# Four query projections in a row: reordering the calls of the mixer stage in a hybrid decoder layer

## The chip, the cores and the metric

The kernel runs on one core of a Trainium2 chip. The metric is the device time of one execution in microseconds (us), as the median of three runs. One further execution was profiled; its time and its trace are shown below.

## What is computed

One decoder layer over 512 tokens and a model width of 1024, in float32:

```
h = x + 0.5 * swiglu(rmsnorm(x), W1)
n = rmsnorm(h);  z = n @ w_in
aq, ak, av, gq, gk, gv, glr, gog = split(z)
A: aq, ak = rope(rmsnorm per head); window attention (128) with sinks, blocks of 128 queries
B: gated linear attention, 4 heads: log_alpha from glr, chunked recurrence over q, k, v;
   rmsnorm(out) * silu(gog)
h = h + concat(A, B) @ w_out
h = h + 0.5 * swiglu(rmsnorm(h), W2)
out = h + sigmoid(rmsnorm(h) @ W_g) * rmsnorm(p @ W_p)
```

The change lies in the mixer: the attention A and the recurrence B, between the two feed-forward networks.

## The kernel before

Every weight is split into a high and a low part (`Weights.split`: a cast on ScalarE, L130, a subtraction on VectorE, L131), and every large product is three matmuls (`mm3`, L187). The split tiles live in a ring of five buffers per part (`ringp`, tags whi and wlo); raw weights are loaded by SP into two buffers. A projection of 128 tokens onto 512 columns (`gemm_ts`, L295) is 24 matmuls and reads four ring tiles.

The mixer handles the 512 tokens in four blocks of 128, called 0 to 3.

- `queries(n)` (L611): projects the queries of block n (aq, 24 matmuls), copies them to SBUF and squares them on ScalarE (L617, L540), sums the squares per head on VectorE (L542, L543), takes the power -0.5 on GpSimd (L262, tile rs_q), scales (qn, L624) and rotates them on VectorE (L551 to L554), transposes them on TensorE (qtr, L629) and copies the result (qT, L631).
- `scores(n)` (L636): scores sc on TensorE in two halves, mask added on VectorE (e, L651), row maximum (mx, L653), exponentials on ScalarE (L660), reciprocal of the sum (rd, L664), scaling of e on ScalarE (L666).
- `weighted(n)` (L669): transposes e (pt, L677), copies it (pb, L679), multiplies with the values (pv) and copies into araw (L686).
- `gla_qk(j)`: the recurrence's queries and keys. `gla_decay()` (L787): the decays qb and kd, and three pairs of transposes of kd (kdt, L801).
- `gla_level(i)` (L733), seven levels of the chunk (64, 32, ... 1): X on VectorE (L739, L740), its exponential on ScalarE (L741), two products on VectorE (L742, L743), a product gr on TensorE, and a masked copy into Ac on VectorE (fill, L767; for level 64 a copy on ScalarE). `gla_diagonal()` does the same for the diagonal (gd).
- `gla_v(t)` (L705) and `gla_gate(t)` (L712): the value projection gv and the gate projection gog of block t, 24 matmuls each. `gla_state`, `gla_out`, `gla_silu` and `gla_mix` finish the recurrence, and wo projects back.

Two things set the order. First, the program is handed to a list scheduler when it is built (`schedule_with_timeline_sim=True`, L1004): an instruction that is ready goes into its engine's queue, and among several that are ready the one that stands earlier in the program goes first. Each engine then runs its queue in that order. Second, tiles of one tag share a fixed number of buffers, and an instruction that writes a new tile needs a free one:

- psA, two PSUM banks: kvr, gqk, aq of blocks 0 and 1, gv, gog.
- psG, two PSUM banks: cum, aq of blocks 2 and 3 (L614), qtr, kdt, pv, dS, otr.
- psD, two pairs of banks: sc, gr, pt, gd, o.
- w4, four SBUF buffers: la and lb, then At (two, until the end of the recurrence), kd, X.
- sm, sixteen small tiles: sums, scales, maxima, denominators.
- e, two buffers; pb, two; qT, four, later used by the gates.

The order of the calls is written out at L860 to L900, and the change touches that list alone.

Of the kernel before, what the change touches and what calls it, by code (L numbers as in the profile page):

```python
# [140 lines left out]
def hymba_kernel(tc, A, out):  # L141
# [12 lines left out]
    def psA(name):  # L154
        return psp.tile([P, 512], F32, name=name, tag="psA", bufs=2)
# [14 lines left out]
    def psD(name):  # L170
        return halls["D"][1].tile([P, 2, 512], F32, name=name, tag="psD", bufs=2)
# [3 lines left out]
    def psG(name):  # L175
        return psp.tile([P, 512], F32, name=name, tag="psG", bufs=2)

    def w4(name):
        return w4p.tile([P, 1024], F32, name=name, tag="w4")

    def small(name, n):
        return smp.tile([P, 16], F32, name=name, tag="sm", bufs=16)[:, :n]

    def mm(o, l, r, start, stop_, **kw):
        nc.tensor.matmul(o, lhsT=l, rhs=r, start=start, stop=stop_, **kw)  # L185
# [106 lines left out]
    def tokens(t):  # L292
        return slice(t * P, (t + 1) * P)

    def gemm_ts(ps, xT, t, tiles):  # L295

        n = len(tiles)
        for j, (wh, wl) in enumerate(tiles):
            for i in range(2):
                k = 2 * j + i  # L300
                mm3(ps, (xT[0][:, k, tokens(t)], xT[1][:, k, tokens(t)]), (wh[:, i, :], wl[:, i, :]),
                    k == 0, k == 2 * n - 1)
# [228 lines left out]
    def t2(name):  # L531
        return mp.tile([P, 512], F32, name=name, tag="t2", bufs=6)

    def heads(x):
        return x.rearrange("p (a d) -> p a d", d=64)

    def head_scale(src, name):

        sq = t2(f"sq_{name}")
        nc.scalar.activation(sq, src, AF.Square)  # L540
        ss = small(f"qs_{name}", 8)
        nc.vector.reduce_sum(ss, heads(sq), AX.X)  # L542
        nc.vector.tensor_scalar_add(ss, ss, 64.0 * EPS)  # L543
        return rms_scale(ss, 8, f"q_{name}")

    def rotate(x, tab, wide, name):

        t1 = t2(f"r1_{name}")
        tt = t2(f"r2_{name}")
        cs, sn = tab  # L550
        nc.vector.tensor_mul(wide(t1, 0, 64), wide(x, 0, 64), cs(0, 64))  # L551
        nc.vector.tensor_mul(wide(tt, 0, 32), wide(x, 32, 32), sn(0, 32))
        nc.vector.tensor_mul(wide(tt, 32, 32), wide(x, 0, 32), sn(32, 32))
        nc.vector.tensor_add(t1, t1, tt)  # L554
        return t1
# [55 lines left out]
    def queries(n):  # L611
        if not aq_tiles:
            aq_tiles.extend(W.get(("aq", 0, k)) for k in (0, 2, 4, 6))
        ps = (psA, psG)[n // 2](f"aq{n}")  # L614
        gemm_ts(ps, nTm, n, aq_tiles)
        aq = t2(f"aq_{n}")
        nc.scalar.copy(aq, ps)  # L617
        rs = head_scale(aq, f"q{n}")
        qn = t2(f"qn{n}")
        qv = qn.rearrange("p (h g d) -> p g h d", h=4, g=2)  # L620
        src = aq.rearrange("p (g h d) -> p g h d", h=4, g=2)
        rb = rs.unsqueeze(2).broadcast_to([P, 8, 64])
        for g in range(2):
            nc.vector.tensor_mul(qv[:, g], src[:, g], rb[:, 4 * g:4 * g + 4, :])  # L624
        qr = rotate(qn, [lambda a, m, x=x: x[:, n, a:a + m].unsqueeze(1).broadcast_to([P, 8, m]) for x in rtab[0]],
                    lambda x, a, m: heads(x)[:, :, a:a + m], f"q{n}")
        ps = psG(f"qtr{n}")
        for k in range(4):
            nc.tensor.transpose(ps[:, tokens(k)], qr[:, tokens(k)], idn)  # L629
        qT = mp.tile([P, 512], F32, name=f"qT{n}", tag="qT", bufs=4)  # L630
        nc.scalar.copy(qT, ps)  # L631
        qTs[n] = qT.rearrange("p (a c) -> p a c", a=4)
# [3 lines left out]
    def scores(n):  # L636

        k0 = (n - 1) * P if n else 0
        nk = 256 if n else 128
        e = mp.tile([P, 8, 256], F32, name=f"e{n}", tag="e", bufs=2)  # L640
        eg = e.rearrange("p (g a) c -> p g a c", g=2)
        mxt = small(f"mx{n}", 8)
        den = small(f"den{n}", 8)
        for a in range(2):
            sc = psD(f"sc{n}_{a}").rearrange("p g (a c) -> p g a c", a=2)
            for b in range(2):
                for g in range(2):
                    gs = slice(g * 64, g * 64 + 64)
                    mm(sc[:, g, b, :nk], qTs[n][gs, 2 * a + b, :], kT[gs, k0:k0 + nk], True, True)
            half = eg[:, :, 2 * a:2 * a + 2, :nk]  # L650
            nc.vector.tensor_add(half, sc[:, :, :, :nk],  # L651
                                 amask[:, 256 - nk:].unsqueeze(1).unsqueeze(1).broadcast_to([P, 2, 2, nk]))
            nc.vector.reduce_max(mxt.rearrange("p (g a) -> p g a", g=2)[:, :, 2 * a:2 * a + 2], half, AX.X)  # L653
        negm = small(f"nm{n}", 8)
        nc.vector.scalar_tensor_tensor(negm, mxt, -1.0, nsink, ALU.mult, ALU.min)
        es = small(f"es{n}", 8)
        nc.vector.tensor_add(es, negm, sink)
        nc.scalar.activation(es, es, AF.Exp)
        for a in range(8):
            nc.scalar.activation(e[:, a, :nk], e[:, a, :nk], AF.Exp, bias=negm[:, a:a + 1],  # L660
                                 accum_out=den[:, a:a + 1])
        nc.vector.tensor_add(den, den, es)
        rden = small(f"rd{n}", 8)
        nc.vector.reciprocal(rden, den)  # L664
        for a in range(8):
            nc.scalar.activation(e[:, a, :nk], e[:, a, :nk], AF.Copy, scale=rden[:, a:a + 1])  # L666
        es_[n] = e

    def weighted(n):  # L669

        e = es_.pop(n)
        kbs = (0, 1) if n else (0,)
        pbs = []
        for kb in kbs:
            pt = psD(f"pt{n}_{kb}")
            for a in range(8):
                nc.tensor.transpose(pt[:, a // 4, tokens(a % 4)], e[:, a, kb * P:(kb + 1) * P], idn)  # L677
            pb = mp.tile([P, 2, 512], F32, name=f"pb{n}_{kb}", tag="pb", bufs=2)
            nc.scalar.copy(pb, pt)  # L679
            pbs.append(pb)  # L680
        pv = psG(f"pv{n}")
        for kb in kbs:
            for g in range(2):
                mm(pv[g * 64:g * 64 + 64, :], vr[:, n - len(kbs) + 1 + kb, g * 64:g * 64 + 64], pbs[kb][:, g],
                   kb == 0, kb == kbs[-1])
        nc.scalar.copy(araw[:, :, tokens(n)], pv.rearrange("p (a c) -> p a c", a=4))  # L686
# [18 lines left out]
    def gla_v(t):  # L705
        if not gv_tiles:
            gv_tiles.extend(W.get(("gv", 1280, k)) for k in (0, 2, 4, 6))
        ps = psA(f"gv_{t}")
        gemm_ts(ps, nTm, t, gv_tiles)
        nc.scalar.copy(gv[t], ps)  # L710
# [22 lines left out]
    def gla_level(li):  # L733
        s = LEVELS[li]
        X = w4(f"X{s}")
        Xv, bv, kv, qv = (x.rearrange("p (n c) -> p n c", c=2 * s) for x in (X, bF, kF, qF))
        ref = bv[:, :, s - 1:s].broadcast_to([P, 512 // s, s])
        lo, hi = slice(0, s), slice(s, 2 * s)
        nc.vector.tensor_sub(Xv[:, :, lo], ref, bv[:, :, lo])  # L739
        nc.vector.tensor_sub(Xv[:, :, hi], bv[:, :, hi], ref)  # L740
        last_exp[0] = nc.scalar.activation(X, X, AF.Exp)  # L741
        nc.vector.tensor_mul(Xv[:, :, lo], Xv[:, :, lo], kv[:, :, lo])  # L742
        nc.vector.tensor_mul(Xv[:, :, hi], Xv[:, :, hi], qv[:, :, hi])  # L743
        both = psD(f"gr{s}")
        psv = [both[:, p].rearrange("p (n c) -> p n c", c=64) for p in range(2)]
        for n in range(8):
            if s == 64:
                for p in range(2):
                    pr = slice(p * 64, p * 64 + 64)
                    mm(psv[p][0:64, n, :], X[pr, n * P:n * P + 64], X[pr, n * P + 64:n * P + P], True, True)  # L750
            else:
                quarters(n, psv, X, X)
        if s == 64:
            for p in range(2):
                nc.scalar.copy(At[p][0:64, :, 64:128], psv[p][0:64])
        else:
            fill(li - 1, both)
# [102 lines left out]
    gla_clear()  # L860
    for j in range(4):
        gla_qk(j)
    queries(0)
    gla_decay()
    queries(1)
    scores(0)
    gla_level(0)
    queries(2)
    scores(1)
    gla_level(1)  # L870
    weighted(0)
    queries(3)
    gla_level(2)
    scores(2)
    weighted(1)
    gla_v(0)
    gla_level(3)
    scores(3)
    weighted(2)
    gla_v(1)  # L880
    gla_level(4)
    weighted(3)
    gla_v(2)
    gla_level(5)
    gla_v(3)
    gla_level(6)
# [138 lines left out]
```

## Time and profile before

| | us |
|---|---|
| median of three runs | 1019.29 (1017.42 to 1019.44) |
| profiled execution, its own time | 1019.78 |
| its span, first to last instruction | 1018.0 |
| TensorE busy | 976.7 (96%) |
| VectorE busy | 640.6 (63%) |
| ScalarE busy | 402.1 (40%) |
| GpSimd busy | 46.5 (5%) |

Times in the rows are counted from the start of the span. The mixer runs from about 395 to 565 us. A busy time of TensorE counts pipelined matmuls and includes time at a low clock, so it is no measure of peak; where TensorE is not busy at all, it waits.

### The profile page before, as it was taken

The numbers are of one execution on the slowest core, as the hardware profiler recorded it, in microseconds if no ns is written. First come the engines' busy times: TensorE is split into PE (matmuls) and PEld (weight loads), VectorE is DVE, ScalarE is ACT, GpSimd is POOL, SyncE is SP. The second block draws the span as 40 slices with busy tenths as digits, with TensorE's granted clock in tenths as the row PEclk, the third lists the DMA queues.
The fourth block names the chain that finished last, engine by engine and source line by source line (L and its number), as shares of the span: only waits on it lengthen the run. The fifth ranks groups of instructions, "written<-read, shape, count | busy, mean of one in ns | idle before, by whom it ended". The sixth has DMA issues, their size and how long they took to land.

```text
span 1018.0 us, 12357 instructions
## 1 busy us (share of the span) xinstructions
PE 976.7 (96%) x5090; PEld 809.3 (79%) x5090; DVE 640.6 (63%) x807; ACT 402.1 (40%) x588; POOL 46.5 (5%) x58
## 2 busy tenths in 40 slices
PE   6999999999999989967999999999999999999898
PEld 5888888888888868855778879888888888888687
DVE  6485757667576675476655554667566675767653
ACT  6354333333323333564773443343323333233341
POOL 2400000000000000110001100000000000000110
PEclk9899999999999998987999999999999999999999
DMA  7843315133150142300231435243250422402231
GB/s 247 287 171 124 124 41 166 42 124 124 47 172 11 54 135 77 131 1 1 83 84 46 142 96 214 84 147 101 80 168 1 165 83 83 145 1 104 83 114 52
DMA packets 73083, 105.78 MB, mean 104 GB/s; under 512 B 5681, under 2 KB 55106, under 8 KB 73026
## 3 DMA queue, kind: packets, MB, share of 16 engines
q1 hardware_dynamic: 70722, 96.60, 28.6%
q0 software_dynamic: 2304, 8.39, 2.2%
q8 instruction: 40, 0.66, 0.3%
q14 instruction: 17, 0.14, 0.0%
HBM read 98.69 MB, written 6.29 MB: 103 GB/s over the span
## 4 chain that ended last, share of the span: by engine, by line
PE 89%; DVE 6%; DMA 2%; POOL 1%; issue 1%; ACT 1%; SPq 0%; POOLq 0%
PE pu L185 24%; PE pg L185 23%; PE pd L185 20%; PE pgt L185 4%; PE wo L185 4%; PE gog L185 2%; PE gqk L185 2%; PE gv L185 2%; PE aq L185 2%; PE kvr L185 1%; DMA h<-in_x_dram 1%; DMA wraw<-in_ffn_w_gate_dram 1%; PE pv L185 1%; PE o L185 1%; DVE h L322 1%
## 5 line engine op out<-in xcount | busy, mean ns | idle before, releaser
L130 ACT CAST whi<-wraw 128x1024 fp32r<-128x1024 f32 (+1 forms) x130 | 134.4, 1040 | 217.1 <-PE pd L185 151.4
L131 DVE TENSOR_TENSOR wlo<-wraw,whi 128x1024 fp32r<-128x1024 f32 (+1 forms) x126 | 151.7, 1208 | 71.2 <-ACT whi L130 70.1
L185 PE MATMUL pg<-nhi_f,whi 128*128 128x512 f32 (+1 forms) x384 | 142.8, 374 | 2.1 <-ACT nhi_f L255 2.1
L185 PE MATMUL pg<-nlo_f,whi 128*128 128x512 f32 (+1 forms) x384 | 143.6, 374 | 0.0
L185 PE MATMUL pu<-nlo_f,whi 128*128 128x512 f32 (+1 forms) x384 | 143.3, 373 | 0.0
L185 PE MATMUL pu<-nhi_f,wlo 128*128 128x512 f32 (+1 forms) x384 | 143.3, 373 | 0.0
L185 PE MATMUL pu<-nhi_f,whi 128*128 128x512 f32 (+1 forms) x384 | 143.1, 373 | 0.0
L185 PE MATMUL pg<-nhi_f,wlo 128*128 128x512 f32 (+1 forms) x384 | 143.0, 373 | 0.0
L185 PE MATMUL pd<-whi,ahi 128*128 128x512 f32 x312 | 122.4, 392 | 4.4 <-DVE nlo_mix L256 2.2
L185 PE MATMUL pd<-wlo,ahi 128*128 128x512 f32 x312 | 121.9, 391 | 0.0
L185 PE MATMUL pd<-whi,alo 128*128 128x512 f32 x312 | 119.9, 391 | 0.0
L322 DVE SCALAR_TENSOR_TENSOR h<-pd,h 128x512 f32<-128x512 f32 x116 | 76.8, 687 | 36.9 <-PE pd L185 36.9
L185 PEld LDWEIGHTS pg<-nhi_f,whi 128*128 128x128 f32 x384 | 72.8, 190 | 15.0 <-ACT nhi_f L255 2.5
L185 PEld LDWEIGHTS pg<-nlo_f,whi 128*128 128x128 f32 x384 | 73.0, 190 | 12.6 <-DVE nlo_f L256 0.2
L185 PEld LDWEIGHTS pu<-nhi_f,wlo 128*128 128x128 f32 x384 | 73.1, 190 | 12.5
L185 PEld LDWEIGHTS pu<-nlo_f,whi 128*128 128x128 f32 x384 | 73.0, 190 | 12.5
L185 PEld LDWEIGHTS pg<-nhi_f,wlo 128*128 128x128 f32 x384 | 72.9, 190 | 12.5
L185 PEld LDWEIGHTS pu<-nhi_f,whi 128*128 128x128 f32 x384 | 73.0, 190 | 12.4
L362 DVE TENSOR_TENSOR cb<-pu,sg 128x512 f32<-128x512 f32 x44 | 30.4, 690 | 74.3 <-PE pu L185 73.7
L130 ACT CAST whi<-draw 128x1024 fp32r<-128x1024 f32 x35 | 36.7, 1053 | 100.4 <-PE pu L185 54.7
L130 ACT CAST whi<-wpr 128x1024 fp32r<-128x1024 f32 x35 | 36.9, 1053 | 98.6 <-PE pu L185 59.0
L185 PEld LDWEIGHTS pd<-whi,ahi 128*128 128x128 f32 x312 | 58.8, 188 | 17.9 <-DVE nlo_mix L256 2.4
(242 smaller groups left out, 1466.9 us busy)
## 6 DMA issues: line engine op xcount, KB each, us to landing
wraw<-in_ffn_w_gate_dram SPq DMA_DIRECT2D x22, 1024.0 KB, 5.3
wraw<-in_ffn_w_up_dram SPq DMA_DIRECT2D x22, 1024.0 KB, 5.2
wpr<-in_ffn_w_down_dram SPq DMA_DIRECT2D x10, 1024.0 KB, 5.6
draw<-in_ffn_w_down_dram SPq DMA_DIRECT2D x10, 1024.0 KB, 5.2
wraw<-in_w_in_dram SPq DMA_DIRECT2D x8, 1024.0 KB, 5.0
wraw<-in_ple_w_gate_dram SPq DMA_DIRECT2D x4, 1024.0 KB, 4.9
h<-in_x_dram SPq DMA_DIRECT2D x4, 512.0 KB, 8.5
emb_d<-eo POOLq DMA_DIRECT2D x4, 512.0 KB, 10.8
```

Of the source, the lines that this page charges most:

```text
L130: nc.scalar.copy(hi, v)
L131: (nc.gpsimd if u in (2, 3) else nc.vector).tensor_tensor(lo, v, hi.bitcast(F32), op=ALU.subtract)
L185: nc.tensor.matmul(o, lhsT=l, rhs=r, start=start, stop=stop_, **kw)
L322: nc.vector.scalar_tensor_tensor(hs, x, 0.5, hs, ALU.mult, ALU.add)
L362: nc.vector.tensor_mul(cb[:, half].rearrange("p a c -> p (a c)"), pu, sg)
```

## The change

The four calls of `queries` stand together directly behind the four calls of `gla_qk`, ahead of `gla_decay`. The calls of `gla_v` follow earlier ones by one step: `gla_v(0)` stands ahead of level 2 instead of ahead of level 3, `gla_v(1)` ahead of `scores(3)`, `gla_v(2)` ahead of `weighted(3)`. The gates stay last. No function changes.

```diff
     for j in range(4):
         gla_qk(j)
-    queries(0)
+    for n in range(4):
+        queries(n)
     gla_decay()
-    queries(1)
     scores(0)
     gla_level(0)
-    queries(2)
     scores(1)
     gla_level(1)
     weighted(0)
-    queries(3)
+    gla_v(0)
     gla_level(2)
     scores(2)
     weighted(1)
-    gla_v(0)
     gla_level(3)
+    gla_v(1)
     scores(3)
     weighted(2)
-    gla_v(1)
     gla_level(4)
+    gla_v(2)
     weighted(3)
-    gla_v(2)
     gla_level(5)
     gla_v(3)
     gla_level(6)
```

## Rows read from the trace of the kernel before

**Rows 1.** The page: busy time of the span, and granted TensorE clock in 40 slices.
```profile
PE 976.7 (96%) x5090; PEld 809.3 (79%) x5090; DVE 640.6 (63%) x807; ACT 402.1 (40%) x588; POOL 46.5 (5%) x58
...
PEclk9899999999999998987999999999999999999999
```

**Rows 2.** Windows: stretch, its length, busy us of each engine, granted clock, DMA.
```profile
440.00:443.50 3.50, 3.49 (x16) 2.56 (x14) 3.50 (x8) 2.62 (x4) 0.00 (x0) 1.00 0.00 0
443.50:457.40 13.90, 4.51 (x61) 3.66 (x62) 13.45 (x28) 8.29 (x27) 1.64 (x1) 0.82 0.00 0
457.40:489.80 32.40, 24.83 (x228) 18.10 (x226) 18.48 (x29) 18.94 (x46) 1.64 (x1) 0.81 0.02 4
489.80:538.25 48.45, 47.97 (x534) 35.30 (x534) 30.80 (x43) 33.50 (x75) 2.23 (x2) 1.00 0.29 90
538.25:561.60 23.35, 23.35 (x143) 18.65 (x144) 13.88 (x27) 10.50 (x16) 4.05 (x4) 1.00 0.23 58
```

**Rows 3.** Timeline of TensorE: start, us, instruction, idle time before it.
```profile
443.10 0.39 PE L185 MATMUL gv<-whi,nlo_mix 128*128 128x512 f32 x1
...
446.66 0.44 PE L801 MATMUL kdt<-idn,kd 128*128 128x128 f32 x2
...
456.79 1.09 PE L629 MATMUL qtr<-idn,r_q 128*128 128x128 f32 x4 [8.31 <-DVE den L662]
...
471.20 1.09 PE L677 MATMUL pt<-idn,e 128*128 128x128 f32 x8 [1.23 <-DVE e L651]
473.39 1.16 PE L185 MATMUL gr<-X 64*64 64x64 f32 x64 [1.10 <-ACT pb L679]
478.53 1.11 PE L629 MATMUL qtr<-idn,r_q 128*128 128x128 f32 x4 [3.98 <-DVE r_q L554]
479.57 1.98 PE L185 MATMUL pv<-pb,vr 128*64 128x512 f32 x4
```

**Rows 4.** Timeline of ScalarE: three copies out of PSUM.
```profile
440.81 0.59 ACT L617 COPY aq<-aq 128x512 f32<-128x512 f32 x1 [0.25 <-PE aq L185]
...
447.14 0.37 ACT L802 COPY kdT<-kdt 128x256 f32<-128x256 f32 x1 [1.09 <-PE kdt L801]
...
472.32 1.01 ACT L679 COPY pb<-pt 128x1024 f32<-128x1024 f32 x1 [5.42 <-PE pt L677]
```

**Rows 5.** The chain that ended last, pieces in order of time: start, us, what.
```profile
433.55 0.60 ACT aq L617
...
437.56 0.76 DVE qn L624 x2
...
440.66 0.60 DVE r_q L551
...
457.88 7.76 PE aq L185 x24
...
481.55 6.38 PE aq L185 x24
487.93 1.93 PE sc L185 x16
489.86 5.48 PE gv L185 x23
```

**Rows 6.** Timeline of VectorE: masked scores and maxima of blocks 0 and 2.
```profile
447.86 0.69 DVE L653 TENSOR_REDUCE mx<-e 128x4 f32<-128x512 f32 x1
...
490.33 1.22 DVE L651 TENSOR_TENSOR e<-sc,c_amask 128x1024 f32<-128x1024 f32 x1
...
495.40 2.34 DVE L653 TENSOR_REDUCE mx<-e 128x4 f32<-128x1024 f32 x2
```

**Rows 7.** Timeline of GpSimd: the scale of query block 3.
```profile
493.50 1.64 POOL L262 TENSOR_TENSOR rs_q_q<-qs_q,nhalf 128x8 f32<-128x8 f32 x1 [22.95 <-DVE qs_q L543]
```

**Rows 8.** Groups of instructions of ScalarE, 437 to 565: count, busy, mean ns, idle before.
```profile
L660 ACT ACTIVATE e<-e,nm 128x256 f32<-128x256 f32 (+1 forms) x32 | 15.0, 475 | 0.3 <-DVE nm L655 0.3
L666 ACT ACTIVATE e<-e,rd 128x256 f32<-128x256 f32 (+1 forms) x32 | 12.4, 480 | 0.5 <-DVE rd L664 0.5
```

## Prediction

> **What bounds the kernel now.** The page comes first: TensorE is busy 96% of the 1018.0 us span, and of its 40 slices of granted clock four are below nine tenths: the second, and the 16th, 18th and 19th, which are the mixer [rows 1]. So time can come only from holes in TensorE's work, or from its clock. The windows of the mixer locate them [rows 2]: from 443.5 to 457.4 TensorE is busy 4.51 of 13.90 us while VectorE is busy 13.45; from 457.4 to 489.8 it is busy 24.83 of 32.40. That is 9.4 + 7.6 = 17.0 us idle, and the granted clock there is 0.82 and 0.81. From 489.8 to 561.6 only 0.5 us is idle, at full clock [rows 2]. The stage is thus two regimes: a latency chain on VectorE until 489.8, then TensorE, which has the value and gate projections to fill with.
>
> TensorE's own order shows why it has nothing to do at first [rows 3]. After twelve gv matmuls (443.10) it waits 8.31 us for qtr of query block 1, and starts aq of block 2 straight behind it; it waits 3.98 us for qtr of block 2, and then come pv of block 0 and aq of block 3. Neither aq of block 2 nor pv of block 0 lacked data or a bank: the last kdt was evicted by 447.5, pb was there by 473.3 [rows 4]. They go right behind a qtr because psG (two banks) is given out in the program order of the first write: qtr0, kdt x3, qtr1, aq2, qtr2, pv0, aq3. The bank pairs of psD are given out likewise. gv could not fill the hole: the ring of five weight tiles holds the four aq tiles until aq of block 3 has read them, so only one gv tile exists (2 of 8 k steps, for two banks of psA: 12 matmuls). gv goes on at 489.86, its matmuls 5.48 / 23 = 0.24 us apart [rows 5].
>
> The Trainium skill ("Perfetto Trace Analysis", Identifying Performance Opportunities) reads repeated bubbles as a sign that on-chip memory ran out for the next tile. By that, a free bank would have let aq2 start at 447.5; the rows show both banks free from then and aq2 only behind qtr1, so here it is the order of the grants and not their number.
>
> **The change, part by part.** No instruction is added or removed; four projections and four gv calls change place. New order of grants in psG: qtr0, qtr1, aq2, qtr2, aq3, qtr3, kdt x3, pv0. So aq3 loses pv0 ahead of it, and everything hangs on T, the end of aq3: there the aq weights leave the ring and gv begins to fill without end.
>
> What T is worth. Up to 489.8 the kernel before has done, beyond what must precede aq3, the three kdt pairs (3 x 0.44), pt of block 0 (1.1), one gr (1.2), pv of block 0 (1.98 at the low clock, about 1.1 at the high one) [rows 3] and sc of block 2 (1.9) [rows 5]: 6.6 us, which now lies behind T. What follows is the same work, TensorE bound. So the gain is 489.8 - 6.6 - T = 483.2 - T.
>
> How T comes. The first part is unchanged to about 443.5: decay and level 0 are ready at the same time, and VectorE takes what is ready, so qtr0 stays.
> - qtr1. Before, aq1 is copied from 440.8 on [rows 4] and qtr1 starts at 456.8: 16.0 us. The chain of waits gives what one block needs undisturbed [rows 5]: copy of aq at 433.55 to the end of qn at 438.32, 4.8 us, then the rotation, two operations of 0.60 (the first is the row at 440.66) and two on half the columns, 1.9, together 6.7 us. The other 9 are VectorE's queue, 13.45 of 13.90 us busy. Of this queue two maxima mx of block 0 (0.6 each at their spacing) and four operations of X16 (0.6 each at the same spacing) leave [rows 6]: the first because of the small tiles (below), the second because the buffers of tag w4 are now held by kd until kdt, which stands behind qtr3. Decay, X64, X32 and the two mask additions stay. 456.8 - 3.6 = 453.2; the bounds are 447.5 (undisturbed) and 456.8 (as before).
> - aq2 ends 8.84 us behind the start of qtr1, as before (456.79 to 465.63, where 24 matmuls took 7.76 us, against 24 x 0.24 = 5.7 at the full clock [rows 3, 5]): 462.0. The idle time ahead stays near 4.5 us, so I keep the low clock's price.
> - qtr2. Before: 465.63 to 478.53, 12.9 us. Undisturbed 6.7. The two mx of block 1 (2.3) leave, the mask additions (2.3), a fill (1.2) and X16 stay, part of them while the block is on ScalarE and GpSimd. I take 8, nearer the undisturbed end, since VectorE is far from full there (18.48 of 32.40 [rows 2]): 470.0.
> - aq3: qtr2 and 24 matmuls between 6.38 and 7.76 [rows 5], about 7.4 with the transposes: T = 477.4.
> Gain 483.2 - 477.4 = 5.8 us. By the low bounds (447.5 + 7 + 6.7 + 7 = 468.2) it would be 15; by the high ones (456.8 + 8.8 + 12.9 + 7.4 = 485.9) -2.7.
>
> What is moved behind T. The small per-row tiles (tag sm) are also given out in program order of first writes: the mx of block 2 run only at 495.40, though their scores were masked from 491.5 on, and the scale of query block 3 started on GpSimd at 493.50 [rows 6, 7]. The scales of all four blocks now stand ahead of mx of block 0. So the softmax of block 0 waits until about T + 2 = 479, instead of starting at 447.9, and with it pt0, gr16 and all the later tiles of psD. The cover for this is the filler: 84 gv and 96 gog matmuls, 43 us at 0.24. ScalarE is next in line: its 33.5 us of 489.8 to 538.25 [rows 2], plus the exponentials and scalings of blocks 0 and 1 (half of 15.0 + 12.4 [rows 8]) and some 2 us of copies, make 49, so the last diagonal product cannot end before about 479 + 49 + 3 = 531, against 538.25 now. With TensorE bound to 489.8 + 71.8 - 5.8 = 555.8, this fits.
>
> Costed at nothing: the splits of the gv tiles and the one load that each frees on SP's queue come earlier with T; ScalarE does not have the softmax to do just then (if that cover failed, the three casts and subtractions would cost some 4 us once). GpSimd has only the four scales. wo, the second FFN and the end are shifted as they are.
>
> **The rivals.**
> A, the forecast: T between 472 and 480, gain 3 to 11, 1008 to 1016 us.
> B, the query chain runs undisturbed: T near 469, gain 14, about 1005. For it: queries now precede decay and levels. Against: VectorE and its queue were full at 443 to 457, and lower work that is ready earlier is ahead in the queue whatever its rank.
> C, the four do not stand together on TensorE at all, and nothing moves: aq2 still waits for qtr1 and aq3 for qtr2, with the delays of before; T 482 to 486, gain 1 to -3, about 1020.
> D, slower: the postponed softmax becomes the bound. Place: ScalarE and the psD tiles from T + 2 on. pt0 moves from 471.2 to about 487 (maxima, exponentials and scaling of block 0 take 8 us). If the chain from pt0 to the end of the diagonal product keeps its 67 us (471.2 to 538.25), it ends at 554; of the 23.35 us behind it [rows 2] the gog filling (61 matmuls, 14) is then gone, but its latency of some 15 us is not: 569 against 561.6, about 1027. It decides once the diagonal product ends after 541. For it: everything of the attention is now queued in 50 us of ScalarE, with 10 us to spare. Against: in these 67 us the scores of blocks 2 and 3 waited for aq2 and aq3 (gr16 at 473.4, sc of block 2 at 487.9 [rows 3, 5]); their queries are now long there.
> A rule of the Trainium skill stands with D: "Perfetto Trace Analysis" (Optimization Strategy) advises interleaving regimes whose busiest engines differ, and this change takes interleaving away between projections and softmax. Before, rows 2 show the interleaved stretch at half of TensorE's time and VectorE full, so its interleaving did not keep TensorE fed.
>
> **How the numbers follow.** The profiled execution took 1019.78 us (span 1018.0 and 1.8 around it), 0.5 above the median of the runs, 1019.29. 1019.3 - 5.8 = 1013.5. Chances: A 0.52, B 0.12, C 0.16, D 0.20. About 0.2%, 2 us, is what a measurement tells from no change: faster is A and B, 0.64; same is most of C, 0.14; slower is D and the end of C, 0.22. The range 1005 to 1021.5 takes in A, B's bound and C, and leaves out D and the tail of B. The likeliest case's own range is 1008 to 1016.
>
> **What would show it.** aq of block 2 right behind qtr1 at 450 to 455, aq3 behind qtr2 with no pv between; gv going on near 478; mx of block 0 only behind the fourth scale; kdt behind qtr3; idle time of TensorE down from 17 to some 10 us, still with a low clock; the diagonal product at 528 to 538; the last gog matmul near 556. Wrong if gv goes on after 484, if mx of block 0 runs ahead of the fourth scale (then the chain is shorter still), or if TensorE idles more than 3 us between T and the start of wo.

## The result, and the profile after

The changed kernel takes **1031.42 us** (1030.22 to 1032.49, four runs); the kernel before took 1019.12 beside it (1017.42 to 1019.44). The ratio is 1.0124, 95% interval 1.0106 to 1.0141: 12.3 us slower, where 5.8 us faster was forecast. The profiled execution took 1031.97, with a span of 1030.1.

The page of after: busy time of each engine, and the granted clock in 40 slices, against [rows 1].

```profile
PE 981.4 (95%) x5090; PEld 813.1 (79%) x5090; DVE 641.4 (62%) x807; ACT 401.4 (39%) x588; POOL 46.5 (5%) x58
...
PEclk9899999999999989988999899999999999999999
```

The span grew by 12.1, TensorE's busy time by 4.7, so its idle time by 7.4. VectorE, ScalarE and GpSimd are busy for the same time within 0.8 us. Where the idle time lies is shown by the windows of after, four with the bounds of the last four of [rows 2] and one that goes on behind them (stretch, length, busy us of PE, PEld, DVE, ACT, POOL, granted clock, DMA):

```profile
443.50:457.40 13.90, 6.12 (x63) 4.78 (x63) 9.94 (x19) 3.29 (x5) 1.64 (x1) 0.83 0.00 0
457.40:489.80 32.40, 24.65 (x165) 19.59 (x163) 18.79 (x31) 9.95 (x19) 3.27 (x2) 0.86 0.19 65
489.80:538.25 48.45, 46.55 (x354) 35.54 (x355) 28.50 (x41) 36.05 (x102) 0.00 (x0) 1.00 0.18 44
538.25:561.60 23.35, 18.39 (x255) 11.07 (x253) 14.21 (x19) 20.45 (x36) 0.60 (x1) 0.93 0.39 114
561.60:606.00 44.40, 42.14 (x275) 34.60 (x275) 23.37 (x39) 11.92 (x18) 6.17 (x8) 0.92 0.28 96
```

Up to 489.8 TensorE idles 7.78 + 7.75 = 15.5 us, against 17.0 before. From 538.25 on, where it had hardly idled, it idles 5.0 and 2.3 us, and ScalarE does 20.45 us of work in 23.35, twice what it did there before (10.50). Of these, 9.8 us are attention, of which before had none there: exponentials 1.5, scaling of e 3.3, copies pb 3.9 and araw 1.1. Over 443.5 to 606 the idle time is 24.7 us; before it was 17.6, the 17.4 of [rows 2] and 0.2 in this last stretch:

```profile
561.60:606.00 44.40, 44.22 (x207) 36.34 (x206) 23.16 (x32) 16.80 (x31) 3.84 (x7) 1.00 0.35 121
```

That is 7 us. The clock was 1.00 from 538 to 606 and is now 0.93 and 0.92: an estimate by busy time is 18.39 x 0.07 + 42.14 x 0.08 = 4.7 us, less 1.0 which the better clock up to 489.8 gives back by the same reckoning. By this estimate the two account for 10.7 of the 12.0 us by which the last matmul of wo is later (609.1 before, 621.1 now). Behind wo the shift stays.

TensorE's timeline of after, against [rows 3]:

```profile
454.66 1.12 PE L629 MATMUL qtr<-idn,r_q 128*128 128x128 f32 x4 [5.72 <-DVE r_q L554]
...
473.23 1.12 PE L629 MATMUL qtr<-idn,r_q 128*128 128x128 f32 x4 [5.80 <-DVE r_q L554]
...
480.79 0.62 PE L185 MATMUL gv<-whi,nhi_mix 128*128 128x512 f32 x2
...
490.31 0.63 PE L629 MATMUL qtr<-idn,r_q 128*128 128x128 f32 x4 [1.20 <-DVE r_q L554]
490.77 0.38 PE L801 MATMUL kdt<-idn,kd 128*128 128x128 f32 x2
...
497.21 0.60 PE L801 MATMUL kdt<-idn,kd 128*128 128x128 f32 x4
497.65 0.82 PE L677 MATMUL pt<-idn,e 128*128 128x128 f32 x6
...
561.91 1.16 PE L185 MATMUL gd<-gqT,gkT 64*64 64x64 f32 x64 [1.36 <-DVE Ac L767]
```

Three things are to be seen. First, the four projections stand together in the program and not on TensorE: it still waits for a rotated query block ahead of qtr1 (5.72) and qtr2 (5.80). Second, gv goes on at 480.79 instead of 489.86. Third, the chain that the softmax opens, from pt of block 0 to the diagonal product gd, starts at 497.65 instead of 471.20 and ends at 563.07 instead of 538.25. Meanwhile the gates, the last filler, are gone (the last gog matmul starts at 540.8 of after; before, at 561.4):

```profile
L185 PE MATMUL gog<-whi,nlo_mix x32: 388/390/504, 509.5 to 540.8; 128*128 128x512 f32 x32
```

The timelines of GpSimd and VectorE of after, against [rows 6, 7], show what the softmax of block 0 stood behind:

```profile
483.25 1.64 POOL L262 TENSOR_TENSOR rs_q_q<-qs_q,nhalf 128x8 f32<-128x8 f32 x1 [15.24 <-DVE qs_q L543]
```

```profile
483.07 0.68 DVE L653 TENSOR_REDUCE mx<-e 128x4 f32<-128x512 f32 x1
485.55 1.23 DVE L131 TENSOR_TENSOR wlo<-wraw,whi 128x1024 fp32r<-128x1024 f32 x1 [1.79 <-ACT whi L130]
486.69 0.68 DVE L653 TENSOR_REDUCE mx<-e 128x4 f32<-128x512 f32 x1
...
487.96 0.16 DVE L655 SCALAR_TENSOR_TENSOR nm<-mx,nsink 128x8 f32<-128x8 f32 x1
...
494.60 0.17 DVE L655 SCALAR_TENSOR_TENSOR nm<-mx,nsink 128x8 f32<-128x8 f32 x1
...
497.85 0.69 DVE L739 TENSOR_TENSOR X<-bT 128x512 f32<-128x512 f32 x1 [2.88 <-PE kdt L801]
...
519.53 0.17 DVE L655 SCALAR_TENSOR_TENSOR nm<-mx,nsink 128x8 f32<-128x8 f32 x1
...
535.12 0.17 DVE L655 SCALAR_TENSOR_TENSOR nm<-mx,nsink 128x8 f32<-128x8 f32 x1
```

The first maximum of block 0 (447.86 before) runs at 483.07, right behind the sum of squares of query block 3 and as its scale, the fourth, begins on GpSimd. The X of a later level waits for kdt, which stands behind qtr3. The negated maxima nm, one a block, are 6.6, 24.9 and 15.6 us apart. The scores of a later block need a pair of banks of psD, which the pt and gr ahead of them must free first.

### The profile page after: what moved, and what is told of

Read it like the earlier page. It is cut to its first block, busy times and chain, and to the rows that moved or that the text cites. A ratio compares the mean times of both kernels' runs of the same rounds, so it can differ in the third digit from the quotient of the medians.

```text
span 1030.1 us, 12357 instructions
## 1 busy us (share of the span) xinstructions
PE 981.4 (95%) x5090; PEld 813.1 (79%) x5090; DVE 641.4 (62%) x807; ACT 401.4 (39%) x588; POOL 46.5 (5%) x58
## 4 chain that ended last, share of the span: by engine, by line
PE 82%; DVE 6%; ACT 6%; DMA 3%; POOL 1%; issue 1%; SPq 0%; POOLq 0%; ACTq 0%
PE pu L185 23%; PE pg L185 23%; PE pd L185 20%; PE pgt L185 4%; PE wo L185 3%; PE gqk L185 2%; PE aq L185 2%; ACT e L660 1%; DMA wraw<-in_w_out_dram 1%; ACT whi L130 1%; DVE wlo L131 1%; PE kvr L185 1%; PE pe L185 1%; DMA wraw<-in_ffn_w_gate_dram 1%; ACT e L666 1%
## 5 line engine op out<-in xcount | busy, mean ns | idle before, releaser
L185 PEld LDWEIGHTS pu<-nhi_f,wlo 128*128 128x128 f32 x384 | 73.0, 190 | 12.4
L185 PEld LDWEIGHTS pg<-nhi_f,wlo 128*128 128x128 f32 x384 | 72.9, 190 | 12.4
```

## The experiments

In the expectations, **S** puts the loss on the postponed softmax (the small tiles of tag sm, given out in program order); the rivals are named where they stand. Each was measured beside the kernel before (medians 1019.39, 1019.57 and 1018.85 in the three groups of four).

**Which part of the change costs.** First the queries together as changed, the gv calls back at their old places:

```diff
     weighted(0)
-    gla_v(0)
     gla_level(2)
     scores(2)
     weighted(1)
+    gla_v(0)
     gla_level(3)
...
```

> One part of the change alone: the four queries together, gv calls where they stood before. Theory S: mx of block 0 stays behind the fourth scale (near 483), time 1028 to 1034, as the whole change. Theory H: most of the loss comes back, 1017 to 1023, since the splits of gog and w_out rank later again. Theory K: as S.

Measured: 1030.22 (ratio 1.0108, 1.0084 to 1.0133). mx of block 0 starts at 482.3 and gd at 560.8, about as in after. H is refuted: the loss did not come back. Then the other part alone: the order of before with the three gv calls one step earlier (the diff is against before).

```diff
     queries(3)
+    gla_v(0)
     gla_level(2)
     scores(2)
     weighted(1)
-    gla_v(0)
     gla_level(3)
...
```

> The other part of the change alone: queries, decay and scores as before, gv calls one step earlier. Theory O: the loss is in the queries, so within 2 us of the kernel before, 1017 to 1021.5. Theory H: 1024 or more.

Measured: 1016.74 (0.9979, 0.9967 to 0.9990), 2.8 us faster than before by the medians, 2.1 by the ratio. So the whole loss is in the place of the queries. The gv part is a small gain in the order of before; beside the grouped queries it brings none (1031.42 with it, 1030.22 without). Last, a smaller dose: queries 0 to 2 together, `queries(3)` left behind `weighted(0)`, gv as changed.

```diff
-    for n in range(4):
-        queries(n)
+    queries(0)
+    queries(1)
+    queries(2)
     gla_decay()
...
     weighted(0)
+    queries(3)
     gla_v(0)
```

> A smaller dose of the change: queries 0 to 2 together, queries(3) behind weighted(0) as before, gv calls as changed. Theory O: mx of block 0 waits for the third scale (near 466 instead of 483) and kdt for qtr of block 2 (near 473 instead of 490), the chain starts some 15 us earlier than with the whole change, time 1017 to 1024. Theory that any grouping of the queries costs the same: 1028 or more.

Measured: 1019.19 (1.0009, 1.0000 to 1.0018). mx of block 0 comes at 464.6 and kdt at 473.7. The groups of gd in this kernel and in before (ns of one, first and last start) give the end of the chain:

```profile
L185 PE MATMUL gd<-gqT,gkT x64: 218/218/267, 539.5 to 540.4; 64*64 64x64 f32 x64
```

```profile
L185 PE MATMUL gd<-gqT,gkT x64: 218/218/267, 537.1 to 538.0; 64*64 64x64 f32 x64
```

The softmax starts 17 us later than in before, the chain ends 2.4 us later, the gates still run until 563, and the time is that of before. Against e8, which has the gv part alone, the three grouped queries lose some 2.5 us; the fourth loses the other 12.

**What about the queries costs.** The five small tiles of the softmax get a tag of their own, everything else as changed:

```diff
+    def soft(name, n):
+        return mp.tile([P, 16], F32, name=name, tag="so", bufs=16)[:, :n]
-        mxt = small(f"mx{n}", 8)
+        mxt = soft(f"mx{n}", 8)
```

(den, nm, es and rd likewise.)

> The changed order, but the five small tiles of scores (mx, nm, es, den, rd) get a tag of their own (16 buffers), so that they no longer stand behind the four scales of the queries in one tag. Theory S (the tag order of the small tiles makes the softmax of block 0 wait for the fourth scale, and the chain from pt of block 0 to the diagonal product keeps its 65 us): mx of block 0 goes back from 483 to 448 to 452, pt of block 0 from 497.7 to 466 to 476, the diagonal product ends at 530 to 543 instead of 563, time 1006 to 1018. Theory H (the gv calls and the weight splits that they pull ahead use up the fill and block the queues of ScalarE and VectorE behind loads of w_out): the softmax starts early, but the diagonal product still ends after 552, time over 1024. Theory K (kd keeps a buffer of tag w4 until kdt behind qtr of block 3, so the levels from 8 on are late): X8 still not before 485, time over 1026.

Measured: 1027.65 (1.0079, 1.0056 to 1.0102). Of 12 us only 3.8 came back: S, as I had stated it, missed, and K had it (over 1026, X of level 8 not before 485). Its timelines of TensorE and VectorE show why:

```profile
467.79 1.06 PE L680 MATMUL pt<-idn,e 128*128 128x128 f32 x8 [1.32 <-DVE e L654]
474.51 1.13 PE L185 MATMUL gr<-X 64*64 64x64 f32 x32 [5.66 <-DVE X L746]
475.58 1.11 PE L632 MATMUL qtr<-idn,r_q 128*128 128x128 f32 x4
...
483.44 0.44 PE L185 MATMUL gr<-X 64*64 64x64 f32 x10
484.24 0.34 PE L185 MATMUL gr<-X 64*64 64x64 f32 x6
487.46 0.44 PE L185 MATMUL gr<-X 64*64 64x64 f32 x10
489.19 0.34 PE L185 MATMUL gr<-X 64*64 64x64 f32 x6
489.46 1.13 PE L185 MATMUL sc<-kT,qT 64*128 64x256 f32 x8
```

```profile
470.53 0.68 DVE L742 TENSOR_TENSOR X<-bT 128x512 f32<-128x512 f32 x1
...
505.20 0.69 DVE L742 TENSOR_TENSOR X<-bT 128x512 f32<-128x512 f32 x1 [2.75 <-PE kdt L804]
```

pt of block 0 is early again (467.79), but the next product of the chain, gr of level 16, takes until 489.5. kd holds a buffer of w4 until kdt, and kdt stands behind qtr3. So X of level 16 shares one buffer with level 32 and is begun at 470.53, against 450.91 before. Only half of its product then runs ahead of qtr2; the other half comes behind aq3, in pieces between gv matmuls. sc of block 2 follows it in psD, and at 505.20 the X of level 4 still waits for kdt. gd comes at 550.90. The other hold alone: small tiles as changed, `gla_decay` called behind the first query block, which puts kdt early.

```diff
-    for n in range(4):
-        queries(n)
+    queries(0)
     gla_decay()
+    queries(1)
+    queries(2)
+    queries(3)
```

> The changed order, but gla_decay directly behind queries(0), as before; kdt then stands behind qtr of block 0 in psG and kd is free early. Theory K: X8 is written at 475 to 480 instead of 497.9, the diagonal product ends 8 us or more earlier, time 1017 to 1024. Theory S: X8 is early, but gr8 stands behind pt of block 1 in psD anyway; the diagonal product ends within 3 us of 563, time 1028 to 1033.

Measured: 1027.42 (1.0072, 1.0039 to 1.0104). kdt at 443 to 446, but mx of block 0 at 482.2, pt at 495.3 and gd at 558.1. By the median 4.0 us are back, less than K and more than S had forecast; but the six runs lie between 1023.53 and 1031.31, and the traced one took 1030.1, so how much this edit brings alone is not well told. Then both edits in one kernel:

> The changed order with e1 and e3 together: small tiles of scores in a tag of their own, decay directly behind queries(0). Only pv of block 0 is then left behind qtr of block 3 (psG). Theory O: pv of block 0 stays near 500 and holds the two buffers of pb, so pt of block 1 and the levels behind it in psD stay late; better than e1 by 1 to 5 us, 1022 to 1027, still slower than before. If instead small tiles and kd were all of it: 1019 or less.

Measured: 1019.38 (0.9998, 0.9987 to 1.0008). The time is that of before, where I had expected part of the loss to stay (against e8, with its early gv, 2.6 us are still missing). Its timeline of TensorE:

```profile
456.44 1.09 PE L632 MATMUL qtr<-idn,r_q 128*128 128x128 f32 x4 [8.31 <-DVE den L665]
...
470.61 1.09 PE L680 MATMUL pt<-idn,e 128*128 128x128 f32 x8 [1.22 <-DVE e L654]
472.81 1.16 PE L185 MATMUL gr<-X 64*64 64x64 f32 x64 [1.10 <-ACT pb L682]
...
542.70 1.16 PE L185 MATMUL gd<-gqT,gkT 64*64 64x64 f32 x64 [0.48 <-DVE Ac L770]
```

pt and gr of level 16 stand within 0.6 us of [rows 3], the wait of 8.31 is there again, and gd starts 5.6 us later than in before, with the gates still there to cover it (the last gog starts at 557.7). So the queries cost by **two** holds on one chain, sm and w4: with either one left the chain stays late (gd at 558.1 or 550.9, against 542.7 without both), and removing both is worth 12.0. By the medians the two alone bring 3.8 + 4.0; whether they add up is open, since the runs of e3 spread so far. That it is through w4 that the early decay acts is read from the traces: the edit moves kdt, and with it the end of kd.

Is it the number of small buffers, or who is handed them? The mixer's small tiles in one tag of 32:

```diff
+    def many(name, n):
+        return mp.tile([P, 16], F32, name=name, tag="many", bufs=32)[:, :n]
```

> The changed order, with 32 buffers instead of 16 for the mixer's small tiles, all in one tag as before. Theory S: it is the order within the tag, not the number: mx of block 0 stays at 483 behind the fourth scale, time within 2 us of 1031. Theory N (the sixteen buffers ran out): mx of block 0 comes before 465, time under 1024.

Measured: 1031.30 (1.0111, 1.0087 to 1.0136), mx of block 0 at 483.3. More buffers changed nothing.

**What would feed TensorE.** What held aq of blocks 2 and 3 was the order of psG [rows 3]; here all four go through psA, in the changed order:

```diff
-        ps = (psA, psG)[n // 2](f"aq{n}")
+        ps = psA(f"aq{n}")
```

> The changed order, but all four aq take their banks from psA (before: blocks 2 and 3 from psG), so that aq2 no longer stands behind qtr1 and aq3 no longer behind qtr2. Theory O (what stands behind the transposes of the last query block in the tags sm, psG and w4, that is the softmax of block 0, kdt and pv of block 0, starts the long chain of the bank pairs too late; the fill is then gone before the chain ends): the four projections run nearly back to back, the last ends before 470 instead of 480.8, its qtr before 478 instead of 490.3, mx of block 0 before 472 instead of 483, the diagonal product ends before 552, time 1010 to 1021. Theory H (the fill is used up too early, whatever the chain does): the fill ends still earlier, the diagonal product not, time 1028 or more.

Measured: 1010.22 (0.9912, 0.9893 to 0.9931). Its windows, with the bounds of [rows 2]:

```profile
443.50:457.40 13.90, 13.90 (x76) 11.29 (x75) 12.02 (x20) 5.88 (x8) 1.64 (x1) 1.00 0.33 97
457.40:489.80 32.40, 31.54 (x300) 23.76 (x299) 24.57 (x45) 22.72 (x63) 3.28 (x2) 1.00 0.12 39
489.80:538.25 48.45, 45.45 (x366) 32.35 (x364) 32.89 (x45) 40.12 (x88) 0.00 (x0) 1.00 0.29 78
538.25:561.60 23.35, 18.45 (x266) 14.67 (x265) 13.06 (x24) 7.06 (x12) 3.64 (x4) 0.85 0.09 25
```

The holes of 9.4 and 7.6 us are 0 and 0.9, at full clock; 3.0 and 4.9 us have opened behind them, at a clock of 0.85 in the last. The postponed maxima come at 467.2, qtr3 at 472.4 and gd at 541.9. That is 21 us faster than after. The same line in the order of before, queries interleaved and gv late:

> The calls in the order of the kernel before, aq of blocks 2 and 3 in psA as in e5. If the bank tag is what makes the gain of e5 (aq2 and aq3 no longer behind qtr1 and qtr2, so that they fill the hole of 8.3 us): aq2 starts near 441 instead of 457.5 and gv goes on before 475, time 1004 to 1014. If the changed order is needed for it: aq2 still after 450, time 1015 or more.

Measured: 1010.43 (0.9915, 0.9896 to 0.9934). The four aq are done by 453 with no idle time of TensorE between them. The chain of waits of this kernel has 45 of their 96 matmuls in one piece:

```profile
438.12 10.24 PE aq L185 x45
```

So the bank tag alone brings 8.4 us in the order of before, and 21.2 in the changed one. The two kernels differ in gv as well as in the queries, so their equal times do not say that the order of the queries is free; e10 below sets that right. With the own small tiles added to the changed order:

> As e5, and the small tiles of scores in a tag of their own as in e1. Theory O: mx of block 0 near 449 and qtr of block 3 before 478, so the chain of the bank pairs starts near 470 and is not stopped by pv of block 0; the diagonal product ends before 543, time 1004 to 1016. Theory H: 1026 or more.

Measured: 1010.62 (0.9933, 0.9910 to 0.9955), no further gain; with the early decay as well:

> The changed order with all three: aq in psA, small tiles of scores in their own tag, decay behind queries(0). Theory O (starting the softmax and the levels earlier shortens the chain of the bank pairs while there is fill): the diagonal product ends before 538, time 1002 to 1009, below e5. If ScalarE or TensorE's fill bounds the stage by now: within 2 us of e5's 1010.2.

Measured: 1007.91 (0.9889, 0.9875 to 0.9904), 2.3 below the tag alone; the two intervals overlap. And the tag in the order of before with gv one step earlier, the two gains of e9 and e8:

> As e9, and the gv calls one step earlier as in e8. If the gain of e8 (2.8 us) and that of e9 add up: 2 to 4 us below e9. If both fill the same hole: within 1.5 us of e9.

Measured: **1006.26** (1004.08 to 1006.62; ratio 0.9868, 0.9852 to 0.9885), the fastest of all. It is 4.2 us below the tag alone, where gv by itself was worth 2.8. Against e5, which differs from it in the place of the queries alone, it is 4.0 us faster (0.9868 against 0.9912, intervals apart): with the wait for psG gone, interleaved queries are still better, by 4.0 us instead of 14.7 (1016.74 in e8 against 1031.42 in after). Its windows:

```profile
443.50:457.40 13.90, 13.90 (x76) 11.20 (x75) 12.02 (x19) 7.58 (x11) 1.64 (x1) 1.00 0.35 115
457.40:489.80 32.40, 29.99 (x294) 22.19 (x293) 26.98 (x49) 24.97 (x67) 3.27 (x2) 1.00 0.05 17
489.80:538.25 48.45, 44.37 (x520) 31.76 (x519) 29.37 (x39) 35.33 (x78) 0.60 (x1) 0.99 0.36 98
538.25:561.60 23.35, 23.35 (x138) 18.49 (x135) 15.21 (x31) 8.71 (x16) 6.16 (x8) 0.95 0.08 26
```

The hole ahead of qtr1 is closed, and none is open from 538.25 to 561.6; 2.4 and 4.1 us are idle between. gd starts at 533.5, and the last gog matmul at 539.9.

## Why the prediction was wrong

- **What bounds the kernel.** Right: the holes stood behind two query blocks, by the order of the grants in psG. e5 and e9 closed the larger one by another tag alone. The Trainium skill says that a gap that repeats can mean a want of memory for the next tile ("Perfetto Trace Analysis", Identifying Performance Opportunities). For sm, too, no run here agrees: e4 doubled the buffers, and the time stayed at 1031.30.
- **T.** The order on TensorE came as written: aq2 behind qtr1, aq3 behind qtr2 with no pv between, kdt behind qtr3, mx behind the fourth scale. The times were a little optimistic: qtr1 at 454.66 (453.2 forecast), qtr2 at 473.23 (470.0), gv going on at 480.79 (477.4). The largest miss, 2.1 us, is from the end of aq2 (463.1) to qtr2: I took 8, it was 10.1, because a fill and two operations of X16 stood inside the block's rotation on VectorE (470.12 to 472.49), where I had hidden part of them under ScalarE and GpSimd. So the gain at T is 483.2 - 480.8 = 2.4 us and not 5.8. The idle time up to 489.8 fell to 15.5 us, where I had some 10.
- **The step that failed** is the price of "what is moved behind T". I took the chain from pt0 to gd as work that ScalarE could do in 49 us without a pause, and ended it at 531. From 489.8 to 538.25 ScalarE was busy 36.05 us and idle 12.4 (the windows of after). The chain is one of latencies: a block's softmax passes through VectorE, ScalarE, TensorE and back and holds a psD pair meanwhile. It took 65.4 us (497.65 to 563.07), against 67 before (471.20 to 538.25), and 63 to 73 in every other run but e1, where the second hold stood inside it (84). So a softmax that started 35 us later ended the chain 25 us later, at 563 and not at 531, when the filler had run out at 541.
- **The argument against D** was false. I said that in those 67 us the scores of blocks 2 and 3 had waited for their queries, so that the chain would shrink. The queries were early now, and the chain shrank by 1.6 us. The 67 us should have been taken as the chain's own, and D's 0.20 made much larger.
- **D's size.** D began the chain at 487 and ended gd at 554; it began at 497.65 and ended at 563.07. T accounts for 3.4 of the 10.6. Most of the rest is the way from the first maximum to pt0, 14.6 us where D had 8. The rows of VectorE and TensorE above show part of it: the second half of mx0 stood behind the subtraction of a weight split until 486.69, and kdt and gv stood ahead of pt0 on TensorE (the scaling of block 0 on ScalarE was done at 495.5). D's mechanism gave 1027; measured were 1031.
- **A step half seen.** That kd keeps a buffer of w4 until kdt was in the prediction, as relief for VectorE ahead of qtr1. That it also keeps X from the levels that stand in psD between two blocks was not; e1 and e7 show that the loss stays as long as either hold is left.
- **"gv costed at nothing"** was nearly right: its move alone is worth 2.8 us (e8), and beside the grouped queries nothing (e2).
- **The rule set beside D**, the Trainium skill's advice to interleave regimes whose busiest engines differ ("Perfetto Trace Analysis", Optimization Strategy), agrees with the 12.3 us lost by the changed order. With the wait for psG out of the way and gv early in both, it still does, by less: 1010.22 grouped (e5), 1006.26 interleaved (e10).

What stays open: how much of the loss is due to weight splits that stand ahead of the softmax in the queues of ScalarE and VectorE. The largest such wait is read from the timeline of ScalarE of after, 5.72 us for a load of w_out, with pb next in its queue:

```profile
516.06 1.05 ACT L130 CAST whi<-wraw 128x1024 fp32r<-128x1024 f32 x1 [5.72 <-DMA wraw<-in_w_out_dram]
517.01 1.01 ACT L679 COPY pb<-pt 128x1024 f32<-128x1024 f32 x1
```

It was not tested by itself. Nor was kd in a buffer of its own, without another order of the calls.

## What to carry to other kernels

Where tiles of a tag are handed out in program order, moving a call moves all its tiles in every tag: for each tag, list who now stands behind the moved tiles, and follow each of those to the end of its own chain. Price a postponed chain by its measured length in the trace, not by the busy time of its engines, unless a row shows which wait inside it goes away; a filler that starts earlier is worth nothing once it runs out ahead of that chain. Before reordering calls to close a hole, ask which shared buffer put the hole there: one line that gave aq another tag brought 8 us in the old order and 21 in the new one.

## What was not expected of the hardware

Clock was lost where TensorE did not idle long. From 561.6 to 606 of after it was busy 42.14 of 44.40 us, and the granted clock was 0.92, against 1.00 with 44.22 busy before. Windows of after and a row of TensorE place the loss:

```profile
563.07:590.00 26.93, 24.98 (x141) 20.32 (x141) 13.77 (x25) 6.60 (x11) 6.17 (x8) 0.87 0.19 71
```

```profile
571.00:574.00 3.00, 1.48 (x6) 1.26 (x8) 1.96 (x4) 0.41 (x1) 0.92 (x2) 0.71 0.00 0
574.00:577.00 3.00, 3.00 (x16) 2.33 (x15) 1.38 (x2) 0.60 (x1) 0.82 (x1) 0.50 0.01 3
577.00:580.00 3.00, 3.00 (x18) 2.34 (x16) 2.41 (x5) 0.59 (x1) 1.01 (x1) 0.66 0.00 0
```

```profile
572.52 1.22 PE L185 MATMUL o<-gv,At 128*128 128x128 f32 x4 [1.75 <-DVE on L841]
```

From 563.07 to 590 TensorE is busy 93%, and a mean of 0.87 between the two levels, 2.4 and 1.2 GHz, is about a quarter of the stretch at the lower one, some 7 us. They lie together: the clock is 1.00 from 563.07 to 571, falls about where TensorE comes out of an idle time of 1.75 us, stays at the lower level through 3 us in which it is busy throughout, and is 1.00 again from 580 on. The loss is thus paid behind the gap, by work that does not wait. In e10, too, the stretch from 538.25 to 561.6 has TensorE busy throughout and a clock of 0.95, behind a stretch with 4.1 us idle. In after the late chain came with two losses, the waits and a lower clock in and behind them; that the one caused the other is argued from the rows and not shown by a run.
